# Row normalisation by the sum of absolute values: tiles of 12 rows per partition in four buffers, in place of 16 rows in three

## The chip, the cores and the metric

The kernel runs on one core of a Trainium2 chip. A core has a vector engine (DVE), a scalar engine (ACT), a matrix engine (PE, unused here), GpSimd (POOL, only some constants here) and a sync engine (SP). They are separate, each runs its own list of instructions, and they wait for each other by semaphores. Data come from the chip's main memory (HBM) into the on-chip memory SBUF, which has 128 partitions, and go back by DMA transfers. The core's transfers run on 16 DMA engines. An instruction on SP or ACT issues a transfer and goes on; each of these two engines has its own DMA queue.

The metric is the device time in microseconds (us) of one execution. For comparisons the median of several executions is used. The profile is of one execution; its span runs from the first to the last instruction.

## What is computed

```python
x = np.random.randn(32, 512, 1024).astype(np.float32)

def reference(x):
    sums = np.sum(np.abs(x), axis=-1, keepdims=True)
    return (x / (sums + 1e-8)).astype(np.float32)
```

There are 32 x 512 = 16384 rows of 1024 floats. Every row is divided by the sum of the absolute values in it. 67.11 MB are read and 67.11 MB are written.

## The kernel before

A tile holds R = 16 rows in each of the 128 partitions, 64 KB per partition, 8.39 MB in all. The rows of a partition lie one after the other in HBM, so a partition's part of a tile is one piece of 64 KB. There are 8 tiles (numbered from 0), in a pool of three buffers: the load of tile 3 needs the buffer of tile 0, and so waits until tile 0's store is done.

The order is written out by hand (`manual_schedule`), one tile after the other in the loop at the end of the function. For each tile:

- SP issues the load (line 70).
- DVE sums absolute values of all rows of the tile in one instruction (line 40), adds the epsilon (line 47) and takes the reciprocal (line 49). These need the whole tile.
- DVE multiplies the first half of the rows by their reciprocals, in place (line 50). At the same time ACT multiplies the other half, one instruction for each row (line 57).
- ACT issues the store (line 75), once both halves are done.

Since loads are on SP's queue and stores on ACT's queue, a waiting load holds up later loads only, and a waiting store holds up ACT's work for the next tile. The last tile is handled in two parts of 8 rows: two loads, two rounds of arithmetic, two stores ("7a" and "7b" where they are named). The small sums and reciprocals come from a pool of four buffers.

Of the kernel before, what the change touches and what calls it, by code (L numbers as in the profile page):

```python
# [1 line left out]

# [4 lines left out]

FP32 = mybir.dt.float32
EPS = 1e-8


@with_exitstack
def kernel(
    ctx: ExitStack,
    tc: tile.TileContext,
    x: bass.AP,
    out: bass.AP,
):
    nc = tc.nc
    P = nc.NUM_PARTITIONS  # L20

    x_flat = x.flatten_outer_dims()
    out_flat = out.flatten_outer_dims()
    n, d = x_flat.shape

    R = 16
    assert n % (P * R) == 0
    ntiles = n // (P * R)
    BUFS = 3

    x_t = x_flat.rearrange("(n p r) d -> n p r d", p=P, r=R)
    out_t = out_flat.rearrange("(n p r) d -> n p r d", p=P, r=R)

    sbuf = ctx.enter_context(tc.tile_pool(name="sbuf", bufs=BUFS))
    stats = ctx.enter_context(tc.tile_pool(name="stats", bufs=4))

    def normalize(x_tile, r0, k, kv):

        s = stats.tile([P, R], FP32)
        nc.vector.tensor_reduce(  # L40
            out=s[:, :k],
            in_=x_tile[:, r0 : r0 + k, :],
            axis=mybir.AxisListType.X,
            op=mybir.AluOpType.add,
            apply_absolute_value=True,
        )
        nc.vector.tensor_scalar_add(out=s[:, :k], in0=s[:, :k], scalar1=EPS)  # L47
        inv = stats.tile([P, R], FP32)
        nc.vector.reciprocal(out=inv[:, :k], in_=s[:, :k])  # L49
        nc.vector.tensor_mul(  # L50
            out=x_tile[:, r0 : r0 + kv, :],
            in0=x_tile[:, r0 : r0 + kv, :],
            in1=inv[:, :kv].unsqueeze(2).to_broadcast([P, kv, d]),
        )
        for r in range(kv, k):
            row = x_tile[:, r0 + r, :]
            nc.scalar.activation(  # L57
                out=row,
                in_=row,
                func=mybir.ActivationFunctionType.Copy,  # L60
                scale=inv[:, r : r + 1],
            )

    with tc.manual_schedule():
        for i in range(ntiles):
            parts = 2 if i == ntiles - 1 else 1
            k = R // parts
            x_tile = sbuf.tile([P, R, d], FP32)
            for r0 in range(0, R, k):
                nc.sync.dma_start(  # L70
                    out=x_tile[:, r0 : r0 + k, :], in_=x_t[i][:, r0 : r0 + k, :]
                )
            for r0 in range(0, R, k):
                normalize(x_tile, r0, k, k // 2)
                nc.scalar.dma_start(  # L75
                    out=out_t[i][:, r0 : r0 + k, :], in_=x_tile[:, r0 : r0 + k, :]
                )


# [1 line left out]
_INS = ['x']  # L81
_OUTS = [((32, 512, 1024), 'float32')]


# [23 lines left out]
```

## Time and profile before

| what | value |
|---|---|
| time, median of 11 runs | 320.15 us |
| lowest and highest of the 11 | 317.57 and 324.34 us |
| profiled execution, its own time | 321.15 us |
| its span | 319.4 us |
| DVE busy | 211.2 us |
| ACT busy | 68.8 us |
| loads, stores issued | 9 and 9 |
| packets of each of the two queues | 1296 |

The difference between the time and the span, 1.75 us, lies before the first and after the last instruction. In the page's rows of forty digits, each digit is a slice of 8 us and tells in tenths how busy an engine was in it. The DMA row is the mean over 16 DMA engines. A row of the timeline has the start, the duration, the engine, the line of the kernel, the operation, what it writes and reads, and in brackets how long the engine had been idle and for what. A row of the stretches has the stretch, its length, busy time of DVE, ACT and POOL (with the number of instructions), the clock of PE, the DMA share and the GB/s. "To landing" is the time from the issue of a transfer until its completion is signalled.

Two groups of instructions make up nearly all of DVE's time: the reduce of line 40 (17.2 us for 16 rows, 8.7 for 8) and the multiply of line 50 (8.7 us for 8 rows, 4.4 for 4).

### The profile page before, as it was taken

What the parts mean: (1) busy time and instruction counts of PE and PEld (TensorE: products, weight loads), DVE (VectorE), ACT (ScalarE), POOL (GpSimd) and SP (SyncE); (2) the same over time, 40 slices, a digit from 0 to 9 for tenths busy, and PEclk for the clock granted to TensorE, in tenths of its full rate; (3) what the DMA queues carried; (4) which work ended last, traced back from release to release, by engine and by line L of the source; (5) the groups of instructions that cost most, each with busy time, mean ns of one, the idle gap of its engine ahead of it and who ended that gap; (6) DMA issues with size and microseconds to landing.
All of it is one profiled execution on the core that took longest, in us unless ns stands there. A gap on an engine that the chain in (4) does not pass through costs nothing.

```text
span 319.4 us, 198 instructions
## 1 busy us (share of the span) xinstructions
DVE 211.2 (66%) x36; ACT 68.8 (22%) x65; POOL 0.2 (0%) x4
## 2 busy tenths in 40 slices
DVE  0019999999997003999049980599706999942940
ACT  0010090063036000019000280003700036140040
POOL 0000000000000000000000000000000000000000
DMA  9999999999999999999999999999999999999957
GB/s 394 394 394 525 394 394 394 402 509 402 394 517 394 402 460 451 394 419 501 394 402 509 402 394 509 402 403 451 460 394 402 447 431 423 501 410 398 394 222 328
DMA packets 2593, 134.23 MB, mean 420 GB/s; under 512 B 288, under 2 KB 288, under 8 KB 288
## 3 DMA queue, kind: packets, MB, share of 16 engines
q1 hardware_dynamic: 1296, 67.11, 49.2%
q10 hardware_dynamic: 1296, 67.11, 48.6%
q14 instruction: 1, 0.01, 0.0%
HBM read 67.11 MB, written 67.11 MB: 420 GB/s over the span
## 4 chain that ended last, share of the span: by engine, by line
DMA 59%; DVE 33%; another core or an unknown queue 3%; issue 0%; SPq 0%; DVEq 0%; ACTq 0%
DMA x_tile<-in_x_dram 31%; DMA out_dram<-x_tile 28%; DVE s L40 22%; DVE x_tile L50 11%; DVE inv L49 0%; DVE s L47 0%; SPq L70 0%; DVEq L50 0%; ACTq L75 0%
## 5 line engine op out<-in xcount | busy, mean ns | idle before, releaser
L40 DVE TENSOR_REDUCE s<-x_tile 128x16 f32<-128x16384 f32 (+1 forms) x9 | 137.9, 15322 | 94.9 <-DMA x_tile<-in_x_dram 94.9
L57 ACT ACTIVATE x_tile<-x_tile,inv 128x1024 f32<-128x1024 f32 x64 | 67.5, 1136 | 215.8 <-DVE inv L49 215.8
L50 DVE TENSOR_TENSOR x_tile<-x_tile,inv 128x8192 f32<-128x8192 f32 (+1 forms) x9 | 69.7, 7744 | 0.6
L57 ACT ACT_TABLE_LOAD x1 | 1.3, 1283 | 22.5 <-DMA x_tile<-in_x_dram 22.5
L49 DVE RECIPROCAL inv<-s 128x16 f32<-128x16 f32 (+1 forms) x9 | 2.2, 242 | 0.3
L47 DVE TENSOR_SCALAR s<-s 128x16 f32<-128x16 f32 (+1 forms) x9 | 1.6, 174 | 0.3
L92 POOL MEMSET const-bfloat16-1.0<- 128x1 bf16 x1 | 0.1, 102 | 0.0
L92 POOL MEMSET const-uint8-127<- 128x1 uint8 x1 | 0.1, 102 | 0.0
L92 POOL MEMSET const-float32-0.0<- 128x1 f32 x1 | 0.1, 99 | 0.2 <-issue 0.2
L92 POOL MEMSET const-float32-1.0<- 128x1 f32 x1 | 0.1, 99 | 0.0
## 6 DMA issues: line engine op xcount, KB each, us to landing
x_tile<-in_x_dram SPq DMA_DIRECT2D x2, 4096.0 KB, 45.2
out_dram<-x_tile ACTq DMA_DIRECT2D x2, 4096.0 KB, 18.1
x_tile<-in_x_dram SPq DMA_DIRECT2D x7, 45.1
out_dram<-x_tile ACTq DMA_DIRECT2D x7, 43.5
```

Of the source, the lines that this page charges most:

```text
L40: nc.vector.tensor_reduce(out=s[:, :k], in_=x_tile[:, r0 : r0 + k, :], axis=mybir.AxisListType.X, op=mybir.AluOpType.add, apply_absolute_v ...
L47: nc.vector.tensor_scalar_add(out=s[:, :k], in0=s[:, :k], scalar1=EPS)
L49: nc.vector.reciprocal(out=inv[:, :k], in_=s[:, :k])
L50: nc.vector.tensor_mul(out=x_tile[:, r0 : r0 + kv, :], in0=x_tile[:, r0 : r0 + kv, :], in1=inv[:, :kv].unsqueeze(2).to_broadcast([P, kv, d]),)
L57: nc.scalar.activation(out=row, in_=row, func=mybir.ActivationFunctionType.Copy, scale=inv[:, r : r + 1],)
L92: nc = _bacc.Bacc("TRN2", target_bir_lowering=False, num_devices=1)
```

## The change

The tile has 12 rows per partition (48 KB, 6.29 MB) and the pool has four buffers. 128 rows per partition are ten tiles of 12 and a last one of 8, which uses a part of its buffer. The last tile is no longer cut into two parts: every tile has one load, one round of arithmetic and one store. There are 11 loads and 11 stores. A helper `piece` cuts the rows of tile i out of the flat tensors, since the tiles have different heights. Loads stay on SP, stores on ACT, and `normalize` is as before.

```diff
-    R = 16
-    assert n % (P * R) == 0
-    ntiles = n // (P * R)
-    BUFS = 3
 
-    x_t = x_flat.rearrange("(n p r) d -> n p r d", p=P, r=R)
-    out_t = out_flat.rearrange("(n p r) d -> n p r d", p=P, r=R)
+    R = 12
+    BUFS = 4
+    per_partition = n // P
+    assert n % P == 0
+    rows = [R] * (per_partition // R)
+    if per_partition % R:
+        rows.append(per_partition % R)
+
+    def piece(flat, i):
+        a, k = P * sum(rows[:i]), rows[i]
+        return flat[a : a + P * k, :].rearrange("(p r) d -> p r d", p=P)
...
-        for i in range(ntiles):
-            parts = 2 if i == ntiles - 1 else 1
-            k = R // parts
+        for i, k in enumerate(rows):
             x_tile = sbuf.tile([P, R, d], FP32)
-            for r0 in range(0, R, k):
-                nc.sync.dma_start(
-                    out=x_tile[:, r0 : r0 + k, :], in_=x_t[i][:, r0 : r0 + k, :]
-                )
-            for r0 in range(0, R, k):
-                normalize(x_tile, r0, k, k // 2)
-                nc.scalar.dma_start(
-                    out=out_t[i][:, r0 : r0 + k, :], in_=x_tile[:, r0 : r0 + k, :]
-                )
+            nc.sync.dma_start(out=x_tile[:, :k, :], in_=piece(x_flat, i))
+            normalize(x_tile, 0, k, k // 2)
+            nc.scalar.dma_start(out=piece(out_flat, i), in_=x_tile[:, :k, :])
```

## The prediction

> **What bounds the kernel now.** I start with the page: which engine is busy, and whether the DMA engines are.
>
> ```profile
> DVE 211.2 (66%) x36; ACT 68.8 (22%) x65; POOL 0.2 (0%) x4
> DVE  0019999999997003999049980599706999942940
> DMA  9999999999999999999999999999999999999957
> DMA packets 2593, 134.23 MB, mean 420 GB/s; under 512 B 288, under 2 KB 288, under 8 KB 288
> ```
>
> No compute engine is full. DVE has holes, but the DMA row is nines until the last two slices: the kernel is a copy through SBUF with arithmetic beside it. The waits agree (waiter, cause, us in total, times, longest): DVE waits only for loads, and the load queue (SP) only for stores to free a buffer.
>
> ```profile
> DVE s L40 <- DMA x_tile<-in_x_dram: 94.9, 7, 23.3
> SPq L70 <- DMA out_dram<-x_tile: 211.6, 5, 59.5
> ```
>
> Next, stretches of the span: are the waits a loss of transfer time? Last two columns: DMA share and GB/s. A packet counts where it starts, so short rows jump.
>
> ```profile
> 72.50:82.10 9.60, 9.60 (x2) 2.52 (x3) 0.00 (x0) 1.00 1.01 437
> 150.00:290.00 140.00, 93.94 (x17) 30.65 (x30) 0.00 (x0) 1.00 1.00 433
> 302.00:304.00 2.00, 1.90 (x4) 1.14 (x2) 0.00 (x0) 1.00 0.57 246
> 304.00:306.00 2.00, 2.00 (x1) 2.00 (x4) 0.00 (x0) 1.00 0.11 49
> 306.00:308.00 2.00, 1.28 (x1) 1.12 (x2) 0.00 (x0) 1.00 0.08 33
> 308.20:308.40 0.20, 0.00 (x0) 0.00 (x0) 0.00 (x0) 1.00 6.09 2621
> ```
>
> 433 GB/s over 140 us is the full rate: 27.1 GB/s for each of 16 engines, so 2.42 us for a 64 KB packet, 1.81 for 48 KB, 1.21 for 32 KB. 134.22 MB of data need 309.6 us. The first row is the lesson about the waits: tile 2 landed at 72.4, the load of tile 3 was issued only at 82.08 when the store of tile 0 had freed its buffer, so no load was in flight for ten microseconds, and the wire still moved 437 GB/s, all of it stores.
>
> So the only hole is at the end. The timeline there:
>
> ```profile
> 293.69 8.69 DVE L40 TENSOR_REDUCE s<-x_tile 128x8 f32<-128x8192 f32 x1 [10.73 <-DMA x_tile<-in_x_dram]
> 302.86 4.42 DVE L50 TENSOR_TENSOR x_tile<-x_tile,inv 128x4096 f32<-128x4096 f32 x1
> 307.37 0.34 ACTq L75 DMA_DIRECT2D out_dram<-x_tile  x1
> ```
>
> The last half tile lands at 293.67, its store is issued at 307.37. The store before it was issued at 283.05 and took 25.1 us (answer for that one issue), so it landed at 308.15. From 304 to 308 only 164 KB started: 5 packets of 32 KB, where 16 engines at full rate would start 53. One engine fits only 3.3 packets into 4 us, so **about two engines are still at the old store, and about fourteen have nothing**. At 308.3 all 16 start the last store together (2621 GB/s x 0.2 us = 16 packets).
>
> How far do the two lag? From 290 to 308, 5.51 MB started (sum of the two-microsecond rows), 12.7 us at 433 GB/s; spread evenly they start by 302.7 and end near 303.5. The last store's 8 packets of 1.21 us end at 308.3 + 9.7 = 318.0 and it landed at 307.37 + 11.1 = 318.5, so a landing comes 0.5 us after the last byte. The two engines therefore finished at 308.15 - 0.5 = 307.65: a **lag of 4.2 us**, and they idled only 308.3 - 307.65 = 0.65 us before the last store. That is the core of my forecast: fourteen engines have a 5 us hole, but the engines that set the end have almost none.
>
> **The change, part by part.**
>
> Two queues: loads are on SP and stores on ACT before and after (two queues of 67.11 MB each in the page). Worth 0.
>
> Four buffers for three: load i now waits for store i-4. Both hold 48 rows per partition in all. The first store's issue moves from 49.01 to: landing 22.46 less 4 rows x 1.21 us = 17.6, plus the time from landing to store, 26.55 us for 16 rows (22.46 to 49.01) and 13.76 for 8 (269.29 to 283.05), so 20.15 for 12: 37.8, on the wire 0.9 later (as 307.37 to 308.3): 38.7. Then queues alternate. Reads alone need 154.8 us; 36.8 are done by 38.7. Tile 3 lands near 81; store 0 (6.29 MB, 14.5 us alone, 29 shared) lands near 70 and releases load 4, 11 us before load 3 ends. So loads no longer run dry. Worth 0 all the same, since the 72.5 to 82.1 row shows the wire full when they did.
>
> Smaller tiles: DVE per tile by the shapes' means, 17.217 us for the 16-row reduce and 8.686 for 8, so 12.95; multiply 8.692 and 4.425, so 6.56; the two small ones 0.4; some 20.0 us, against 29 us for the pair of transfers. Ten tiles and one of 8 rows (13.6) make 213.6 us, 2 more than now and hidden. ACT does 6 rows of 1.136 us beside the multiply. DVE cover: 9 us per tile.
>
> Four more transfers (22 for 18). Row: load 0 landed at 22.46 and load 1 at 41.85 (40.7 us after issue), 19.4 us apart, exactly 8.39 MB at 433 GB/s; a queued boundary costs 0. Against the change speaks the Trainium skill, "SBUF — State Buffer", section "The DMA setup-cost knee": about 2 us fixed per transfer and the largest single transfer. By that rule +8 us, by the row 0. The row decides, because a second transfer is always queued behind the first; the exposed price is seen only at the ends (load 0: 21.73 - 19.4 = 2.3 us), once in either kernel.
>
> Packet size: 32 KB takes half of 64 KB by the last store (8 packets in 9.7 us), so 48 KB costs no more per byte: 0.
>
> The tail. The last 16 rows came as two halves of 8; now a 12-row tile and one of 8, the same last step (13.76 us to its store, 9.7 us of wire). The queues alternate packet by packet: half tile 7a took 26.8 us (242.5, when tile 6 landed, to 269.29) for 9.7 us of data, 0.36 of the wire, because its 32 KB packets took turns with 64 KB ones. After the change they take turns with 48 KB, 0.40. When does tile 10 land? 118.0 us of reads are left at 38.7: 108.3 at one half, 9.7 at 0.4: 38.7 + 216.6 + 24.2 = 279.5, plus about 2 for the opening packets and up to 4 for lag: 282 to 285. Its store is on the wire by 285 + 13.76 + 0.9 = 299.7. The wire is busy until then with older stores: fast engines would end everything near 1.9 + 309.6 + 2 = 313.5, so the 12-row store ahead ends at 313.5 - 9.7 = 303.8; on the two slow ones 4.2 later, 308. Slack 4 us and 8 us: **the hole closes on all 16 engines**, and the fourteen finish 4 to 5 us early, but nobody can use it: each transfer has 128 data packets and 16 small ones (1296 / 9 = 144), split among the engines beforehand; I assume 8 apiece.
>
> Sum: hole on the slow engines gone, -0.65. Stores start 11 us earlier, so transfers are mixed for 280 us in place of 269; if lag comes with mixing, +0.17. Net **-0.5 us: 321.15 becomes 320.65** (span 318.9 and the same 1.75 around it). The median of the runs shown, 320.15, is 1.0 below that execution; on it the forecast is **319.6**.
>
> The unknown is the lag. By the skill, "DMA: Bandwidth & Descriptors", section "Latency and other measured facts", two engines are usually slower in traces, with a best guess that ties it to software descriptor rings. Both queues here are hardware_dynamic, so by that guess lag should be 0 and the change would save nothing on it either; the rows show two engines late all the same. The cause is open. Bounds: all of it disappears with the new packet layout (-4.2), or it grows with what grows. I take it unchanged, nearest to the row.
>
> **Rivals.**
> 1. *The lag is carried over* (forecast): 319.6, own range 318.6 to 320.8. For it: the same bytes, queues and engines. 0.5.
> 2. *Lag shrinks*: if it hangs on 64 KB packets or the 64 KB address step per partition, both now 48 KB. Then all engines end together: 319.6 - 4.2 = 315.4 at most; half gone, 317.5. For it: the hole on the fourteen closes anyway, so any relief shows directly. Against: nothing in the page ties it to size. 0.32.
> 3. *Lag grows per packet*: 176 data packets per engine in place of 144. At constant lag per packet 4.2 x 176/144 = 5.1, +0.9: 320.5, still no change. It decides from 2.1 us extra, half as much lag again; doubled, 319.6 + 4.2 = 323.8. The place is the slow engines' last store; the price is one for one, as slack covers only fast engines. Against: no packet-size cost in the 32 KB rows. 0.18.
> 4. *The change isn't what it says*: true of the two queues; it leaves rival 1.
>
> **Numbers.** 0.5% is 1.6 us, what a measurement of this kernel can tell from no change. Case 1 gives no change; case 2 mostly faster, case 3 mostly slower. The range 316.2 to 322.4 takes in most of the lag gone (-3.4) and two thirds more of it (+2.8).
>
> **What would show it.** Right: DVE's idle before its reduce stays near 90 us; the windows stay at 433 GB/s to about 300; the last DMA slice is thin, a few engines at work; last store issued 8 us or more ahead of its predecessor's landing. Wrong: the last store issued after its predecessor has landed (tail open), a DMA row below nine in the middle (boundaries cost), or a last slice that is full to its end with a shorter span (lag gone).

## The result and the profile after

The change takes 317.72 us (median of 13 runs, 317.23 to 318.93) against 320.18 us before (median of 48 runs, 317.57 to 324.75). The ratio is 0.9938, with an interval from 0.9918 to 0.9958: faster by 0.6%, or 2.5 us (0.8%) by the medians. The ratio leaves out the slow executions, those more than 1.5% above the fastest of their kernel (15 of the 48 before, none after), and so comes out nearer to 1 than the medians do. The 0.6% is just past the half per cent within which "no change" was the likeliest forecast (319.6 us), and inside its range. The spread shrank as well, from 7.2 us to 1.7. The profiled execution took 318.93 us, its span 317.3; it is the slowest of the 13, as the one before, with 321.15, is 1.0 us above its median.

The page of the changed kernel: busy time, the rows of DVE and DMA, and the packets.

```profile
DVE 212.4 (67%) x44; ACT 69.0 (22%) x65; POOL 0.2 (0%) x4
DVE  0079999998599089719944990797199449939300
DMA  8999999999999999999999999999999999999994
DMA packets 3169, 134.23 MB, mean 423 GB/s; under 512 B 352, under 2 KB 352, under 8 KB 352
```

In the DMA row the thin slice before last ("5" before, now "9") has filled up; only the last one is thin. The waits (waiter, cause, us in total, times, longest) moved little and in opposite directions, DVE's 12 us down and the load queue's 15 us up, while the wire stayed full:

```profile
DVE s L45 <- DMA x_tile<-in_x_dram: 82.6, 9, 18.2
SPq L72 <- DMA out_dram<-x_tile: 226.2, 7, 53.8
```

The end of the timeline: the sums of the last tile, and the issue of its store.

```profile
283.01 8.69 DVE L45 TENSOR_REDUCE s<-x_tile 128x8 f32<-128x8192 f32 x1 [4.89 <-DMA x_tile<-in_x_dram]
296.75 0.34 ACTq L74 DMA_DIRECT2D out_dram<-x_tile  x1
```

And stretches of the span (length, busy time of three engines, PE clock, DMA share, GB/s):

```profile
150.00:290.00 140.00, 98.41 (x21) 31.72 (x30) 0.00 (x0) 1.00 1.00 434
304.00:306.00 2.00, 0.00 (x0) 0.00 (x0) 0.00 (x0) 1.00 1.00 434
306.00:308.00 2.00, 0.00 (x0) 0.00 (x0) 0.00 (x0) 1.00 0.87 377
312.00:313.00 1.00, 0.00 (x0) 0.00 (x0) 0.00 (x0) 1.00 0.61 262
313.00:314.00 1.00, 0.00 (x0) 0.00 (x0) 0.00 (x0) 1.00 0.08 33
314.00:315.00 1.00, 0.00 (x0) 0.00 (x0) 0.00 (x0) 1.00 0.08 33
```

The store of the 12-row tile ahead was issued at 278.21 and took 28.3 us, so it landed at 306.5. The last store was issued 9.8 us before that, and the hole from 304 to 308 is gone. What is left is at the very end: in each of the last two rows one 32 KB packet started (33 GB/s for 1 us), so **one engine** was still at work (one fits less than one such packet into 1 us). By the prediction's own method: from 290 on, 428 x 22 + 262 + 33 + 33 KB = 9.74 MB started, 22.5 us at 433 GB/s; with the same 0.8 us as before for the last packets to end, an even finish would be 313.3. The last store took 19.5 us, landed at 316.25, so the late engine ended at 315.75. The lag, how far the latest engine ends behind that even finish, is 2.4 us; before, it was 4.2.

### The profile page after: what moved, and what is told of

Same layout as the page of the kernel before. It is cut to its first block, busy times and chain, and to the rows that moved or that the text cites. A ratio compares the mean times of both kernels' runs of the same rounds, so it can differ in the third digit from the quotient of the medians.

```text
span 317.3 us, 227 instructions
## 1 busy us (share of the span) xinstructions
DVE 212.4 (67%) x44; ACT 69.0 (22%) x65; POOL 0.2 (0%) x4
## 4 chain that ended last, share of the span: by engine, by line
another core or an unknown queue 45%; DMA 30%; DVE 17%; SPq 1%; issue 0%; DVEq 0%; ACTq 0%
DMA x_tile<-in_x_dram 17%; DMA out_dram<-x_tile 14%; DVE s L45 11%; DVE x_tile L55 6%; SPq L72 1%; DVE inv L54 0%; DVE s L52 0%; DVEq L54 0%; ACTq L74 0%
## 5 line engine op out<-in xcount | busy, mean ns | idle before, releaser
L45 DVE TENSOR_REDUCE s<-x_tile 128x12 f32<-128x12288 f32 (+1 forms) x11 | 138.2, 12564 | 82.6 <-DMA x_tile<-in_x_dram 82.6
L55 DVE TENSOR_TENSOR x_tile<-x_tile,inv 128x6144 f32<-128x6144 f32 (+1 forms) x11 | 70.0, 6364 | 0.4
L54 DVE RECIPROCAL inv<-s 128x12 f32<-128x12 f32 (+1 forms) x11 | 2.5, 225 | 0.9
L52 DVE TENSOR_SCALAR s<-s 128x12 f32<-128x12 f32 (+1 forms) x11 | 1.9, 173 | 0.4
## 6 DMA issues: line engine op xcount, KB each, us to landing
x_tile<-in_x_dram SPq DMA_DIRECT2D x1, 4096.0 KB, 35.7
out_dram<-x_tile ACTq DMA_DIRECT2D x1, 4096.0 KB, 19.5
```

The source lines that it names most:

```text
L45: nc.vector.tensor_reduce(out=s[:, :k], in_=x_tile[:, r0 : r0 + k, :], axis=mybir.AxisListType.X, op=mybir.AluOpType.add, apply_absolute_v ...
L55: nc.vector.tensor_mul(out=x_tile[:, r0 : r0 + kv, :], in0=x_tile[:, r0 : r0 + kv, :], in1=inv[:, :kv].unsqueeze(2).to_broadcast([P, kv, d]),)
```

## The experiments

Two theories were set against each other. The **tail theory**: the hole ahead of the last store is what the change removes, and the late landing of half tile 7b on the slow engines is what opened it. The **lag theory**: a few DMA engines fall behind the others where packets are large, and what the change removes is half of that lag.

The runs were made on different chips, on which the median of the kernel before was 320.2 to 322.8 us. Kernels of one group below share a chip.

**First group** (before: 320.89 us).

`e1_no_sum_7b`: close the hole and leave all else.

```diff
-                normalize(x_tile, r0, k, k // 2)
+                inv = normalize(x_tile, r0, k, k // 2, inv if r0 else None)
```

With an `inv` given, `normalize` only does the multiplications, so 7b is scaled by 7a's reciprocals and its own sums are left out.

> The kernel before, except that the last half tile 7b is scaled by 7a's reciprocals: its own sums are left out. Landing to store falls from 13.76 us to about 4.6, packets and buffers stay at 64 KB and three. Tail theory (the median of before sits 2.4 us above the change because 7b's last landing, in steps of a 64 KB packet, holds back the last store on all 16 engines): the last store is issued near 298.5, before its predecessor has landed, the hole at 304 to 308 closes, and the median is about 317.5 to 318.0, with times in one cluster, as narrow as after's. Lag theory (two engines are 4 us late with 64 KB packets and only 2 us with 48 KB ones): only the 0.65 us gap of the slow engines goes, median about 319.5, times spread as before.

Measured: 320.04 us (318.6 to 322.24), ratio 0.9967 [0.9934, 1.0001]. The timeline's last store comes 7.5 us earlier than before, and the hole after 304 is closed. The later stretches show what came in its place:

```profile
299.83 0.34 ACTq L80 DMA_DIRECT2D out_dram<-x_tile  x1
```

```profile
304.00:306.00 2.00, 0.00 (x0) 0.00 (x0) 0.00 (x0) 1.00 1.10 475
312.00:313.00 1.00, 0.00 (x0) 0.00 (x0) 0.00 (x0) 1.00 0.45 197
313.00:314.00 1.00, 0.00 (x0) 0.00 (x0) 0.00 (x0) 1.00 0.39 164
314.00:315.00 1.00, 0.00 (x0) 0.00 (x0) 0.00 (x0) 1.00 0.38 164
315.00:316.00 1.00, 0.00 (x0) 0.00 (x0) 0.00 (x0) 1.00 0.08 33
316.00:317.00 1.00, 0.00 (x0) 0.00 (x0) 0.00 (x0) 1.00 0.08 33
317.00:318.00 1.00, 0.00 (x0) 0.00 (x0) 0.00 (x0) 1.00 0.08 33
```

The rows go down like stairs: most engines end near 313, where no hole delays them any more; five or so go on (164 KB is 5 packets of 1.21 us each in 1 us), and one goes on to about 319. The time of the kernel is that engine's. (This execution took 322.17 us, 2.1 above the median, so its latest engine is later than in most.) Closing the hole alone brought 0.85 us, with an interval from 2.1 to nothing, where the tail theory asked for about 2.5. The times also stay as wide as before, where it asked for one narrow cluster. The tail theory falls as the whole explanation; the lag is real, with 64 KB packets, three buffers and 16 rows, and no hole.

`e2_halves_16`: every tile of 16 rows in two halves (loads, arithmetic, stores).

```diff
-            parts = 2 if i == ntiles - 1 else 1
+            parts = 2
```

> 16 rows and three buffers as before, but every tile is loaded, worked on and stored in two halves of 8 rows, so all packets are 32 KB and 7b shares the wire with equal packets (one half in place of 0.36). Tail theory: 7b lands earlier, the hole closes, 317.5 to 318.0. Lag theory (lag goes with packet size): lag 1 to 2 us, 317.0 to 317.7. If either the 12-row tile or the fourth buffer were needed: 320.1 as before.

Measured: 317.56 us (317.17 to 317.7), ratio 0.9874 [0.9838, 0.9909]. Neither 12 rows nor a fourth buffer is needed. Both theories had a range that takes in this value.

`e3_8rows_6bufs`: the change with other numbers.

```diff
-    R = 12
-    BUFS = 4
+    R = 8
+    BUFS = 6
```

> The change with 8 rows and six buffers: 16 tiles, 32 transfers, 32 KB packets. Tail theory: hole closed, same as after, 317.3 to 318.0. Lag theory: lag falls with the packet from 2.2 us to about 1.5, so 316.5 to 317.2. A fixed cost of 2 us per transfer: 10 more than after's 22, +20 us.

Measured: 317.32 us (317.12 to 317.84). Ten more transfers than the change's 22 cost nothing that can be seen. It lies in the range of the tail theory and 0.1 above that of the lag theory, so it tells them apart by little.

`e4_12rows_3bufs`: the change with `BUFS = 3`.

> The change with three buffers of 12 rows. Tail theory: loads are held back longer, tile 10 lands near 291 in place of 283, its store is issued near 305, later than the store before it ends on most engines (about 304), so a hole of 1 to 2 us opens: 318.3 to 319.5. Lag theory (only the packet size counts): as after, 317.7.

Measured: 318.73 us (318.46 to 319.18), within what was expected of the tail, and 1.0 above the lag theory's 317.7. The timeline's last store and the stretches around it:

```profile
305.03 0.34 ACTq L74 DMA_DIRECT2D out_dram<-x_tile  x1
```

```profile
304.00:306.00 2.00, 0.95 (x1) 0.73 (x1) 0.00 (x0) 1.00 0.54 229
306.00:308.00 2.00, 0.00 (x0) 0.00 (x0) 0.00 (x0) 1.00 0.70 295
```

The store comes 8.3 us later than in the change, and a hole of 1 to 2 us is open again. So the tail theory is not empty: the fourth buffer is what keeps the tail closed, and that is worth about 1 us (318.73 against 317.72 and 317.91 in two sets of runs of the change; these were on other chips, so the size is less sure than the hole).

**Second group** (before: 322.84 us).

`e5_pad_32k`: the same transfers, tiles, buffers and arithmetic by whole tiles; only the packets get smaller. The rest of the edit adapts the access patterns to the gap.

```diff
-            x_tile = sbuf.tile([P, R, d], FP32)
+            x_pad = sbuf.tile([P, 2, R // 2 * d + 8], FP32)
+            x_tile = x_pad[:, :, : R // 2 * d].rearrange("p h (r d) -> p h r d", d=d)
```

> The kernel before, 16 rows, three buffers, 9 loads and 9 stores, whole-tile arithmetic; only a gap of 32 bytes is put between the two halves of a tile in SBUF, so that a transfer of the same 8.39 MB consists of 32 KB packets in place of 64 KB ones. If the packet size makes the lag: as with halves, 317.3 to 318.0, times in one narrow cluster. If it is the size of the transfer, the tile height, or the buffers: 320 to 321 and wide, as before.

Measured: 317.14 us (317.07 to 317.39), ratio 0.9833 [0.9793, 0.9873]. The page shows the smaller packets: 2192 in each queue in place of 1296, of which 2048 are data in place of 1152 (the others are the 16 small ones of each transfer). The timeline has the last store:

```profile
q1 hardware_dynamic: 2192, 67.11, 49.8%
q10 hardware_dynamic: 2192, 67.11, 49.3%
```

```profile
294.44 0.34 ACTq L86 DMA_DIRECT2D out_dram<-x_pad  x1
```

```profile
312.00:313.00 1.00, 0.00 (x0) 0.00 (x0) 0.00 (x0) 1.00 1.21 524
313.00:314.00 1.00, 0.00 (x0) 0.00 (x0) 0.00 (x0) 1.00 0.01 0
```

The last store comes 12.9 us earlier than before, so the gap closes the hole too; the run to set beside it is the one without 7b's sums, which has no hole either, keeps 64 KB packets, and took 320.04. In the stretches there are no stairs: all 16 engines start a packet in the last full microsecond (524 KB is 16 packets), and none after it. With a gap of 32 bytes the kernel before has a lower median than the change had on either of its chips, and its six times lie within 0.32 us. It keeps the 64 KB step from partition to partition in HBM, so that step is not the cause; nor is the number or size of transfers, the height of the tile, or the number of buffers.

`e6_stores_32k`: only the stores in two of 8 rows.

```diff
-                nc.scalar.dma_start(
-                    out=out_t[i][:, r0 : r0 + k, :], in_=x_tile[:, r0 : r0 + k, :]
-                )
+                for q0 in range(r0, r0 + k, R // 2):
+                    nc.scalar.dma_start(
+                        out=out_t[i][:, q0 : q0 + R // 2, :],
+                        in_=x_tile[:, q0 : q0 + R // 2, :],
+                    )
```

> The kernel before with each tile's store issued as two of 8 rows (32 KB packets); loads stay at 64 KB packets (but for 7a and 7b). Loads then get two thirds of the wire where both queues are full, wait for buffers instead, and 7b lands early: no hole. If the lag comes from 64 KB packets of the loads: still 2 to 4 us of lag, 319.5 to 320.5. If it comes from 64 KB packets of the stores, or from two large ones side by side: 317.3 to 318.0.

Measured: 317.37 us (317.07 to 317.63). Loads of 64 KB packets alone leave no lag worth seeing (the last engine is 0.4 us behind at the end); it takes large packets of the stores, or of both. The run with only the loads in halves, below, tells these two apart.

`e7_one_more_sum`: the change, with the last tile's line 45 done twice (`for _ in range(2)` for that tile).

> The change, with the sum of the last tile (8 rows) done twice: 8.7 us more before the last store. In after the last store is issued at 296.75 and on the wire 0.9 later, 297.7; fast engines finish the store before it near 313.3 - 9.7 = 303.6: 5.9 us of slack, and 8 on the slow one. Expected: 8.7 us more put the store on the wire at 306.4, a hole of 2.8 us on the fast engines, end at 306.4 + 9.7 + 0.5 + 0.9 = 317.5 of span, 319.1 of time, so 1.4 more than after in place of 8.7. If there were no slack: 326.

Measured: 318.57 us (318.0 to 318.93). 8.7 us of work in front of the last store cost 0.7 to 0.9 us (against 317.91 and 317.72, on other chips), where 1.4 was expected. The last store in the timeline, and the stretches:

```profile
304.50 0.34 ACTq L75 DMA_DIRECT2D out_dram<-x_tile  x1
```

```profile
302.00:304.00 2.00, 2.00 (x1) 2.00 (x3) 0.00 (x0) 1.00 0.34 147
304.00:306.00 2.00, 0.41 (x1) 0.25 (x1) 0.00 (x0) 1.00 0.61 262
```

From 302 to 304 only 147 GB/s started, so most engines had run out of stores when this one was issued at 304.50: the hole is back, but shorter than the work added. The rest of the 8.7 us was slack, and part of the hole was time that the late engine would have taken in any case.

`e8_4rows_12bufs`: `R = 4` and `BUFS = 12`.

> The change with 4 rows and twelve buffers: 32 tiles, 64 transfers of 2.1 MB, 16 KB packets. If the lag goes with packet size: 316.9 to 317.3, near the floor of 1.9 + 309.6 + 2 + 0.5 + 0.9 of span. If smaller transfers begin to cost at their boundaries: above 317.7, growing with the number of transfers.

Measured: 318.3 us (318.25 to 318.56). The smallest packets are not the best. One row for the middle of each kernel; first this one, then the change:

```profile
60.00:280.00 220.00, 172.78 (x100) 52.49 (x48) 0.00 (x0) 1.00 1.01 431
```

```profile
60.00:280.00 220.00, 157.31 (x32) 50.75 (x48) 0.00 (x0) 1.00 1.00 434
```

431 for 434 GB/s over the whole transfer is 309.6 x 0.7% = 2 us, more than the lag it saves. The trace also records every packet, and there it is the packet that costs this: the median packet took 0.611 us for 16 KB, 0.912 for 24, 1.213 for 32, 1.815 for 48 and 2.418 for 64, which is 0.602 us for each 16 KB and 9 ns for each packet. An engine moves 512 data packets here and 176 in the change: 336 x 9 ns = 3 us, as an estimate.

**Third group** (before: 320.86 us).

`e9_pad_at_end`: the control for the padded run.

```diff
-            x_tile = sbuf.tile([P, R, d], FP32)
+            x_pad = sbuf.tile([P, R * d + 8], FP32)
+            x_tile = x_pad[:, : R * d].rearrange("p (r d) -> p r d", d=d)
```

> The kernel before with 32 bytes after each 64 KB tile in SBUF in place of between its halves: the buffers move as in the padded run, packets stay at 64 KB. If packet size makes the lag: 320 to 323 and wide, as before. If moved SBUF addresses did it: 317.1.

Measured: 322.37 us (319.74 to 324.96), ratio 1.0015 [0.998, 1.0051]. As slow and as wide as before, within its interval; and its stretches show the hole and the two late engines (66 GB/s for 2 us is 4 packets; one engine fits 1.7):

```profile
302.00:304.00 2.00, 2.00 (x1) 2.00 (x3) 0.00 (x0) 1.00 0.61 262
304.00:306.00 2.00, 2.00 (x1) 2.00 (x2) 0.00 (x0) 1.00 0.15 66
```

So it is the gap inside the tile, which cuts the packets, and not the moved buffers.

`e10_loads_32k`: only the loads in halves.

```diff
-            for r0 in range(0, R, k):
+            for r0 in range(0, R, R // 2):
                 nc.sync.dma_start(
-                    out=x_tile[:, r0 : r0 + k, :], in_=x_t[i][:, r0 : r0 + k, :]
+                    out=x_tile[:, r0 : r0 + R // 2, :],
+                    in_=x_t[i][:, r0 : r0 + R // 2, :],
                 )
```

> The kernel before with each tile loaded in two halves (32 KB packets), stores of 64 KB. Where queues take turns packet by packet, loads get one third of the wire while stores are queued, the last loads land later and the arithmetic on 7a and 7b stands behind tile 6's: a hole of 8 to 10 us before the last store on all engines, 322 to 326. If the wire were shared by bytes, no such hole: 317 to 320. Lag, read in the DMA share ahead of the hole: two or more engines late if 64 KB stores are what makes it.

Measured: 335.39 us (334.23 to 338.13), ratio 1.0453 [1.0388, 1.0518]. The direction was right and the size was not: 9 us above the expected range. The timeline's row for the sums of tile 6, and two stretches beside it:

```profile
268.42 17.22 DVE L40 TENSOR_REDUCE s<-x_tile 128x16 f32<-128x16384 f32 x1 [34.27 <-DMA x_tile<-in_x_dram]
```

```profile
260.00:300.00 40.00, 31.42 (x5) 8.43 (x8) 0.00 (x0) 1.00 0.56 243
280.00:282.00 2.00, 2.00 (x1) 0.00 (x0) 0.00 (x0) 1.00 0.08 33
```

Tile 6 lands at 268.4, in place of 242.5, and DVE has waited 34 us for it; the stores queued before it run out, and then the wire is idle while DVE works through tiles 6, 7a and 7b, one after the other. (This execution took 338.13 us, the longest of the four.)

The lag is what made this so long. For each transfer the trace has 16 completion signals, as many as there are DMA engines. Of tile 6's second half, fifteen had come by 248.9, and the last came at 268.33. From 280 to 282 one engine alone is at work (33 GB/s), and it ends its part of 7b 8.6 us behind the middle of the 16. Without that one engine DVE could have begun 19 us earlier. So large stores beside small loads make an engine late, as both at 64 KB do and as large loads beside small stores do not, each in the one execution profiled.

The turns by packet show on the other engines: 7a's load took 24.1 us (245.3 to 269.4 in the middle of the signals), the first 21.7 beside a 64 KB store. One third of the wire for 21.7 us and all of it for 2.5 is the 9.7 us that its data need; with one half it would be 13.3.

`e11_change_pad_24k`: the same gap in the change, `x_pad = sbuf.tile([P, 2, R // 2 * d + 8], FP32)`, with the access patterns adapted as above.

> The change, with 32 bytes between the two halves of a tile, so that its packets are 24 KB (16 KB in the last tile) in place of 48. If lag is what is left between the change and the floor: 317.0 to 317.3, 0.5 below the change on the same chip and as narrow as the padded 16-row kernel. If the change has no lag left to lose: 317.7.

`e12_change_again`: the change unedited, beside it.

> The change itself, on the chip of the three others: 317.2 to 319, median near 317.7.

Measured: 317.88 us (317.71 to 318.18) with the gap and 317.91 (317.29 to 318.51) without. No gain, which the lag theory had not expected; only the spread got smaller, from 1.2 to 0.5 us. By the 9 ns per packet found above, the gap's 352 data packets per engine in place of 176 cost an estimated 1.6 us, about what the lag gave up. The change's own ratio on this chip is 0.9895 [0.9854, 0.9936].

## Why the prediction held, and which of its steps failed

The time fell into the range because the range had room for rival 2. The forecast itself, rival 1 with 319.6, was 1.9 us too high, and its main case did not come true.

**What bounds it** held: a full wire at 433 GB/s, and only the time in which it isn't full to win. DVE's idle time before its sums stayed near (94.9, then 82.6 us) and cost nothing.

**Queues, boundaries, DVE** held: 0 each. The rule of about 2 us for each transfer that the prediction took from the Trainium skill ("SBUF — State Buffer", section "The DMA setup-cost knee"), 8 us in all, has no trace in any run down to 8-row tiles: 32 transfers took 317.32 us. DVE came to 212.4 us, 213.6 by the sum. The 32 more data packets per engine cost some 0.3 us at 9 ns each, where packet size was priced at 0.

**The tail** held in its places: tile 10 landed at 282.96 (247.26 + 35.7; 282 to 285 by the sum), its store was issued at 296.75 (on the wire by 299.7 by the sum), ahead of its predecessor's end on all engines, and there was slack, about 6 us on the fast engines and 8 on the slow one where the sum had 4 and 8; so the doubled sum's 8.7 us cost only 0.7 to 0.9. The term for the hole, -0.65 us, was measured alone by the run without 7b's sums: -0.85 (nothing to -2.1), a wide interval. One thing was put down to the wrong part: "four buffers" was priced at 0 since the wire is full in the middle, and the tail at the gain. The run with three buffers shows that it is the fourth buffer that brings the last load in time: about 1 us. And the tail does not stand apart from the lag: of the 16 signals of 7b's load in the kernel before, fourteen had come by 280.1, the other two at 288.3 and 293.7. The late engines themselves opened the hole that the fourteen waited in.

**The lag** failed: "I take it unchanged, nearest to the row". In the profiled executions it went from 4.2 to 2.4 us. With the term for the hole that makes -0.65 - 1.8 = -2.45 us; these two executions differ by 2.22, and the medians by 2.46. As each lag is from one execution, and both lie above their medians, the closeness is partly luck. What happened is rival 2 with about half of the lag gone (317.5 by the prediction, 317.72 measured), and the rival's argument against itself ("nothing in the page ties it to size") was the weak sentence: no row of one kernel can tie it to size. Of the two causes rival 2 named, packet size is shown and the address step is ruled out, both by the padded run. Rival 3, a lag that grows with the number of packets, is the wrong way round from 64 to 32 KB.

Where the lag comes from can be followed in the records of the traces. It is not made at the end: counted from the middle of a transfer's 16 signals to the last, it grows from 0.5 us (the store issued at 49.0) over 2.0 (151.5) to 4.4 (283.1) in the kernel before, from 0.8 to 2.7 in the change, and it is never above 1.0 with the gap. And its size fits single packets that take longer. Between 60 and 300 us, 24 packets of the kernel before took over 0.1 us more than is usual for their size, 8.2 us in all, and its two late engines ended the store issued at 283.05 by 3.9 and 4.4 us too late, 8.2 us together. The change had 5 such packets (1.9 us, about what its lag grew by), the padded run 1 (0.2), and no other run with packets of 32 KB or less on both queues more than 2.

**Still open**: why some packets take longer, why next to none do where both queues have packets of 32 KB or less, and which engines are hit. Slow packets alone don't make a lag either: the run with 32 KB stores beside 64 KB loads has 28 slow packets (11.5 us), but most of them come between 249 and 253 us and, as far as packets can be told apart by engine, on all 16 alike, so that no engine ends late.

## What to carry to other kernels

In a kernel like this, where the wire is full, the last of the 16 DMA engines sets the end, and a mean DMA share hides it: cut the last few microseconds into short stretches, count packets, and see whether the row falls at once or in stairs. A hole before the last transfer is worth only what the latest engine idles in it, so close it and even out the engines together. Packet size is a knob of its own (the contiguous piece per partition), apart from the transfer's size: when loads and stores run side by side, keep the stores' packets no larger than the loads', and try 32 KB before adding buffers or changing tile heights. Much smaller ones cost again, packet by packet.

## What the runs showed of the hardware that was not expected

- A gap of 32 bytes inside a tile changes a copy kernel by 1.7% (317.14 against 322.84 us), by cutting 64 KB packets in two. The same gap after the tile changed nothing that could be told (1.0015 [0.998, 1.0051]).
- Times against packet size, for kernels whose tail is closed: 64 KB 320.04 (without 7b's sums), 48 KB 317.72 and 317.91, 32 KB 317.14 to 317.56, 24 KB 317.88, 16 KB 318.3 us. They are from different chips; 24 KB and the second of the 48 KB times were on the same one. Large packets cost by the lag, small ones by 9 ns each.
- Unequal packets share the wire by packets, and the direction matters: loads of 32 KB beside stores of 64 made the kernel 4.5% slower, with one engine 19 us behind the other fifteen in the tile that set the end; stores of 32 KB beside loads of 64 made it 1.6% faster.
- The 48 times of the kernel before lie for the most part in clumps near 317.8, 320.1, 322.6 and 324.6 us, some 2.1 to 2.5 us apart, about a 64 KB packet (2.42 us). That the landing of 7b moves in whole packets would make such steps; it was not tested.
